# Narrower token rows, later weighting and later squares in a retention and HGRN2 step

## The chip, the cores and the metric

The kernel runs on one core of a Trainium2 chip. What counts is the device time of one execution in microseconds (us). Three executions of the kernel before took 1049.72, 1050.12 and 1050.17 us; their median, 1050.12 us, is the time that the change is measured against.

The engines are PE (TensorE, the matrix products; PEld is its loading of weights), DVE (VectorE), ACT (ScalarE), POOL (GpSimd) and SP (SyncE, which here only issues transfers). Each engine works through its own instructions in the order in which they stand, and an instruction that waits holds up all behind it on that engine. Transfers run on 16 DMA engines.

## The reference: what is computed

One mixer layer: normalise, project to eight groups of 512 columns, run two recurrences, weight their outputs, project back, and normalise once more with the final weights.

```python
h = rmsnorm(x, norm_g)
p = (h @ w_in).astype(jnp.float32)
rq, rk, rv, rg, hq, hf, hi, hgate = jnp.split(p, 8, axis=-1)
...
o_ret = head_rmsnorm(o_ret, ret_g) * jax.nn.silu(rg)
...
o_hg, s_hg_new = chunked_decay_recurrence(hq_act, kin, hi, logf, s_hg)
o_hg = head_rmsnorm(o_hg, hg_g) * jax.nn.silu(hgate)
o_cat = jnp.concatenate([o_ret, o_hg], axis=-1)
y = x + o_cat @ w_out
```

`head_rmsnorm` divides each head's output of 128 numbers by the root of its mean square. There are 2048 prompt tokens (width 1024, four heads of 128 for each recurrence) and eight further tokens that go through one decoding step. Every product of float32 matrices is made of three products of rounded halves: with x = xh + xl and w = wh + wl it is xh·wh + xl·wh + xh·wl.

## The kernel before, in words

**Stages.** Stage one (0 to 573 us) normalises the tokens and makes the value, query, key and gate projections and the retention. It goes over 24 blocks of 256 tokens (the eight blocks three times, once for each set of projections), and each block has seven products (`v_pair`, its matmuls in `three`, L352). Before the next block can be scaled, the squares of its tokens have to be summed: `stats_load` (L261) loads the 256 tokens in two halves j = 0 and 1, each as two tiles `xn` of 128x512; `stats_sum` (L267, ACT) squares and sums them; `stats_end` takes the root on POOL (L277, L111, L112); `spread_dg` (L288, DVE) puts the results on a diagonal `dg`, and PE spreads it with the matmul `prs` (L293). In the same stretch the gate weights are loaded (`wgr`, L519), combined on DVE (L505 to L508), stored (`ws1T`, L531) and multiplied with the decoding tokens (`pgd`, L592). The tiles of a pool are used in turn, so that a load into one waits for whatever last used it.

Stage two (573 to 851 us) makes the HGRN projections of the two halves of the tokens, four heads each (`seg_steps`, L996, into `pjfh` and `pjqh`), and runs the recurrence of each head one unit behind the projections. The tokens stand in four blocks of 512, split into `xh` and `xl` (`x_alloc`, `x_split`, L115 and L116), as tiles of 128 partitions x 8 rows of 528 elements, of which blocks 0, 2 and 3 fill 512 and block 1 fills 520 (512 and the eight decoding tokens). The recurrence works in levels (`plh`, L1208, L1253, L1258, and `pah`, L1226); between levels DVE multiplies `kh` and `qqh` (L1178, L1181) and copies a level's result into `Abh` (L1214). `tail_steps` then has, for the two groups of four chunks g = 0 and 1: `kt` (L1075, L1077), `uu` (matmul `puh`, L1083, state update L1091), `oo` (matmul `poh`, L1099 and L1101; squares of the outputs on ACT, L1105; the root on POOL, L111 and L112, into `orsh`; the weighting with root and gate on DVE, L1110, into `obh`) and `tr` (transpose `poth` on PE, L1117; `oth` on ACT, L1119; store to memory, L1120).

Stage three (851 to 1046 us) multiplies the outputs with `w_out`: four token blocks plainly (`py`, L1607) beside the last unit of the recurrence, and the rest with products of sums (`po`, L352). For that the weights are loaded (`wor`, L1476) and split into `woh` (ACT, L1481) and `wol` (DVE, L1482), and the outputs are loaded (`o_load`, L1492, tile `or`) and split into `oc_h` (ACT) and `oc_l` (DVE) by `o_split`. The values and gates of a unit come through four loads (`v`, L1023).

**What sets the order.** PE's order is written out. In stage one a table `after` says behind which of a block's seven products a step is issued. In stages two and three every step has a number between 0 and 1 within its unit, and `merge` puts the lists of steps (projections, levels, and `rest`) together by these numbers; in the last unit they are scaled to 0.57·at for the levels and 0.55 + 0.5·at for `rest`. The order on the other engines comes from a scheduler that may move an instruction ahead of others whose results it doesn't need. `behind(f)` ties what f issues: it is scheduled after the last instruction that DVE, ACT and SP had been given up to that point.

Of the kernel before, what the change touches and what calls it, by code (L numbers as in the profile page):

```python
# [11 lines left out]
F32R = mybir.dt.float32r  # L12
# [6 lines left out]
P = 128  # L19
D = 1024  # L20
KT = D // P
# [20 lines left out]
def step_kernel(ctx, tc, a, out):  # L42
# [67 lines left out]
    def rsqrt_mean(dst, src, n, eps):  # L110
        pool.tensor_scalar(dst, src, 1.0 / n, eps, op0=ALU.mult, op1=ALU.add)  # L111
        pool.tensor_tensor(dst, dst, mhalf[: dst.shape[0], : dst.shape[1]], op=ALU.pow)  # L112
# [11 lines left out]
    def behind(f):  # L124

        last = {}
        for i in reversed(nc.cur_bb.bb.instructions):
            if i.engine in (dve.engine, act.engine, sp.engine) and i.engine not in last:
                last[i.engine] = i
                if len(last) == 3:  # L130
                    break
        with ExitStack() as es:
            for i in last.values():
                es.enter_context(tc.issue_after(i))
            f()
# [40 lines left out]
    x_cur = {}  # L176
    x0p = []

    def x_alloc(blk):
        pl = x0p[0] if blk % 2 else xp  # L180
        x_cur[blk] = tuple(pl.tile([P, KT, 528], F32R, tag=f"x{t}{1 - blk % 2}", name=f"x{t}{blk}") for t in "hl")

    def x_load(blk, kp):
        r = rawp.tile([P, 2, 512], F32, tag="raw", name=f"xr{blk}{kp}")
# [72 lines left out]
    def stats_load(i, j):  # L257
        c = 2 * V_ORDER[i] + j
        st[i, j] = [vq.tile([P, GW], F32, tag="xn", name=f"xn{c}{h}", bufs=2) for h in range(2)]
        for h, r in enumerate(st[i, j]):  # L260
            sp.dma_start(r, a["x_prompt"][0, c * P : (c + 1) * P, h * GW : (h + 1) * GW])  # L261

    def stats_sum(i, j):
        if not j:
            st[i] = sm.tile([P, 4], F32, tag="ms", name=f"ms{V_ORDER[i]}")
        for h, r in enumerate(st[i, j]):
            act.activation(r, r, AF.Square, accum_out=st[i][:, 2 * h + j : 2 * h + j + 1])  # L267
# [618 lines left out]
    for i in range(2, n_tok):  # L886
        after = {n: [] for n in range(7)}
        m, j = i // N_V + 1, i % N_V
        if N_V <= i < 2 * N_V:
            after[3.5 if i > N_V + 1 else 4.5 if i > N_V else 5.5] = [q_flip]  # L890
        if N_V < i <= 2 * N_V:
            after.setdefault(2.5 if i < N_V + 3 else 1.5 if i < 2 * N_V else 2, []).append(q_flip)
        if i in (N_V, 2 * N_V):
            after[4 if i == N_V else 1] += [lambda m=i // N_V: wg_decode_turn(m)]
        if i == 2 * N_V:
            r_begin()
        if i >= 2 * N_V:
            for n, f in r_steps(i - 2 * N_V).items():
                after.setdefault(n, []).extend(f)
        if same(i + 1):  # L900
            for op in ("S1", "S2", "S3", "S4"):
                sop[i + 1, op] = sop[i, op]
        elif i + 1 < n_tok:
            if not spooled(i + 1):
                after[0] += [lambda i=i: spread_dg(i + 1)]
                after[1] += [lambda i=i: spread(i + 1)]
            tied = behind if i >= N_V - 1 else lambda f: f()
            late = 2 if same(i) else 0
            after[2 + late] += [
                lambda i=i, t=tied: t(lambda: tok_ops(i + 1)), lambda i=i, t=tied: t(lambda: s_split(i + 1, 0))  # L910
            ]
            after[4 + late // 2] += [lambda i=i, t=tied: t(lambda: s_split(i + 1, 1))]
        if i + 2 < n_tok and not same(i + 2):
            at = 5 if i % N_V > 2 else 2
            if same(i + 1):
                at = 6
            after[at] += [lambda i=i: tok_load(i + 2)]
        if i + 2 < N_V:
            after[1] += [lambda i=i: behind(lambda: stats_sum(i + 2, 0)), lambda i=i: stats_load(i + 2, 1)]
            after[4] += [lambda i=i: behind(lambda: stats_sum(i + 2, 1)), lambda i=i: stats_end(i + 2)]  # L920
            if i + 3 < N_V:
                after[5] += [lambda i=i: stats_load(i + 3, 0)]
        if N_V <= i + 1 < n_tok:
            after[4] += [lambda i=i: rot_load(i + 1)]
        if i == 2:
            after[0] += [decode_dg]
            after[2] += [decode_spread]
        if m < 3:
            if 2 <= j < 6:
                after[0] += [lambda m=m, k=j - 2: wg_load(m, k)]  # L930
                after[4] += [lambda m=m, k=j - 2: wg_decode(m, k), lambda m=m, k=j - 2: wg_spool(m, k)]
            if j == 7:
                after[0] += [lambda m=m: wg_decode_out(m)]
                for n, (_, op, _) in enumerate(CHAIN):
                    after[n] = [lambda m=m, op=op: wg_fetch(m, op)] + after[n]
        if i >= N_V - 1 and j in (7, 0) and i < n_tok - 1:
            for n, (_, op, _) in enumerate(CHAIN):
                if (n + SPLIT_AT) // 7 == (j + 1) % N_V:
                    after[3 if n == 6 else (n + SPLIT_AT) % 7] += [lambda op=op: behind(lambda: wg_split(op))]
        if i == 2 * N_V + 2:  # L940
            after[0] += [lambda: d_pad(0)]
        hd = i - 2 * N_V - 2
        if 0 <= hd < NH:
            after[3] += [lambda hd=hd: d_load(hd)]
            after[4] += [lambda hd=hd: behind(lambda: d_mul(hd, 0))]
            after[6] += [lambda hd=hd: behind(lambda: d_add(hd))]
        if 0 < hd <= NH:
            after[1] += [lambda hd=hd: d_mm(hd - 1)]
        if i == n_tok - 1:
            after[0] += [w_load]  # L950
            after[0] += [lambda: x_alloc(0), lambda: x_raw.update({(0, kp): x_load(0, kp) for kp in range(4)})]
            for kp, at in enumerate((1.5, 2.5, 3.5, 7)):
                if at > 6:
                    continue
                after.setdefault(at, [])
                after[at] += [lambda kp=kp: behind(lambda: x_split(0, kp, x_raw[0, kp]))]
            after[4] += [w_fetch]
        v_pair(i, after)
# [104 lines left out]
    def tail_steps(half, hd, acol, qcol, vcol, kT, decay, box, eps, gcol, name, ksb, ns):  # L1063
        ob = {}
# [28 lines left out]
        def oo(g):  # L1093
            st = st_tile()
            po = ps_o.tile([P, 4, P], F32, tag="o", name=f"po{name}{g}")
            for j in range(4):
                c = 4 * g + j
                src = box["old"] if c == 0 else st[:, (c - 1) % ns]
                pe.matmul(po[:, j], acol(c), vcol(c), start=True, stop=src is None)  # L1099
                if src is not None:  # L1100
                    pe.matmul(po[:, j], qcol(c), src, start=False, stop=True)  # L1101
            ms = sm.tile([P, 4], F32, tag="oms", name=f"oms{name}{g}")
            for j in range(4):
                jk = pools["tp"].tile([P, P], F32, tag="jk", name=f"jk{name}{g}{j}", bufs=1)
                act.activation(jk, po[:, j], AF.Square, accum_out=ms[:, j : j + 1])  # L1105
            rs = sm.tile([P, 4], F32, tag="ors", name=f"ors{name}{g}")
            rsqrt_mean(rs, ms, P, eps)
            ob[g] = pools["tp"].tile([P, 4, P], F32, tag="ob", name=f"ob{name}{g}", bufs=2)
            for j in range(4):
                dve.scalar_tensor_tensor(  # L1110
                    ob[g][:, j], po[:, j], rs[:, j : j + 1], gcol(4 * g + j), op0=ALU.mult, op1=ALU.mult
                )

        def tr(g):
            pt = ps_tr.tile([P, 4, P], F32, tag="tr", name=f"pot{name}{g}")
            for j in range(4):
                pe.transpose(pt[:, j], ob[g][:, j], ident)  # L1117
            ot = pools["tp"].tile([P, 512], F32, tag="ot", name=f"ot{name}{g}", bufs=2)
            act.activation(ot, pt.rearrange("p a b -> p (a b)"), AF.Copy, scale=ng[:, hd : hd + 1])  # L1119
            pool.dma_start(  # L1120
                o_dram[hd, :, half * HALF + g * 512 : half * HALF + (g + 1) * 512], ot
            )

        return dict(k0=lambda: kt(0), k1=lambda: kt(1), u0=lambda: uu(0), u1=lambda: uu(1),
                    o0=lambda: oo(0), o1=lambda: oo(1), t0=lambda: tr(0), t1=lambda: tr(1))

    def joined(*fs):
        def run():
# [12 lines left out]
    def hgrn_rec(half, h, u):  # L1141
        name = f"h{half}{h}"
# [135 lines left out]
        def last():  # L1278
            if half == 1:
# [3 lines left out]
                  (0.55, lambda: level(3, 0)), (0.68, lambda: level(3, 1)), (0.84, scores3),  # L1283
                  (0.95, t["k0"]), (0.98, t["k1"])]
        rest = [(0.02, begin), (0.13, t["u0"]), (0.28, t["u1"]), (0.43, t["o0"]), (0.47, t["o1"]),
                (0.6, t["t0"]), (0.73, t["t1"]), (0.73, last)]
        if half == 0:
            levels.insert(0, (0.0, lambda: collect(h, u)))
        return levels, rest
# [520 lines left out]
    for i in range(p0, n_pairs):  # L1810
        after = {}
# [98 lines left out]
```

## Time and profile before

| | us |
|---|---|
| median of three executions | 1050.12 (1049.72 to 1050.17) |
| the profiled execution | 1047.95 |
| its span, first to last instruction | 1046.2 |
| PE busy in the span | 1029.7 |
| DVE, ACT, POOL busy | 742.4, 552.6, 130.9 |
| DMA, mean over the span | 233 GB/s |
| granted TensorE clock | 0.999 |

The profiled execution lies 2.2 us below the median and 1.75 us above its own span. A row of a timeline gives the start and the length of an instruction, the engine, the line, the operation, the tiles out<-in, and in brackets how long the engine stood idle before it and what ended that. Neighbouring DVE and ACT instructions overlap by 0.07 to 0.1 us. In rows of waits, "1.5, 1, 1.5" is the total, the number of waits and the longest. "SPq" is SP's queue of transfers: start is when a transfer was issued, not when its data arrived.

### The profile page before, as it was taken

To read this page: it belongs to the slowest core of one execution; us is meant where nothing else is said; L and a number is where in the kernel's file an instruction comes from. 1 tells how busy PE (TensorE), PEld (TensorE's weight loads), DVE (VectorE), ACT (ScalarE), POOL (GpSimd) and SP (SyncE) were. 2 spreads that over 40 slices of the span, in tenths; PEclk is the share of its full clock that TensorE was granted. 3 is DMA by queue.
4 is the path that set the end of the run, shared out by engine and by line. 5 is a ranking of instruction groups with operands and counts; after the bars stand their busy time and mean duration, and the time that the engine had idled before them with its cause. 6 is when DMAs were issued, how large, how long until landed. Compare 5 with 4: busy or idle time off the path is not lost.

```text
span 1046.2 us, 21268 instructions
## 1 busy us (share of the span) xinstructions
PE 1029.7 (98%) x8231; PEld 851.1 (81%) x8231; DVE 742.4 (71%) x1372; ACT 552.6 (53%) x1208; POOL 130.9 (13%) x231
## 2 busy tenths in 40 slices
PE   9999999999999999999999999999999999999997
PEld 7777878887778888888888989897878877888775
DVE  6877567887655875666666776878767587578885
ACT  7954346644334865454555755575555474543241
POOL 0401001000000011111111100011022102311121
PEclk9999999999999999999999999999999999999999
DMA  8689989669876965767785785853876274475652
GB/s 296 210 315 353 312 321 338 244 233 319 274 252 195 328 232 173 195 217 232 217 266 159 260 304 181 271 190 123 269 244 223 67 232 135 155 290 201 232 174 101
DMA packets 145655, 244.08 MB, mean 233 GB/s; under 512 B 10801, under 2 KB 78657, under 8 KB 145425
## 3 DMA queue, kind: packets, MB, share of 16 engines
q1 hardware_dynamic: 137968, 217.68, 62.4%
q0 software_dynamic: 7440, 24.76, 6.2%
q8 instruction: 65, 1.06, 0.4%
q14 instruction: 38, 0.30, 0.1%
q10 hardware_dynamic: 144, 0.26, 0.1%
HBM read 160.22 MB, written 82.44 MB: 232 GB/s over the span
## 4 chain that ended last, share of the span: by engine, by line
PE 86%; DMA 4%; ACT 4%; DVE 4%; issue 1%; POOL 0%; SPq 0%; DVEq 0%; POOLq 0%; ACTq 0%
PE po L352 11%; PE pjfh L996 9%; PE pjqh L996 8%; PE py L1607 4%; PE plh L1208 2%; DMA xn<-in_x_prompt 1%; PE par L735 1%; PE puh L1083 1%; PE poh L1099 1%; PE pur L742 1%; PE por L748 1%; PE por L750 1%; PE poh L1101 1%; PE pv21a L352 1%; PE pv20a L352 1%
## 5 line engine op out<-in xcount | busy, mean ns | idle before, releaser
L1188 ACT ACTIVATE kepth<-kh 128x1024 f32<-128x1024 f32 x24 | 25.4, 1060 | 70.0 <-DVE kh L1178 70.0
L996 PE MATMUL pjfh<-xh,w_h 128*128 128x512 f32 (+2 forms) x160 | 60.2, 376 | 0.0
L996 PE MATMUL pjqh<-xh,w_h 128*128 128x512 f32 (+2 forms) x160 | 60.0, 375 | 0.0
L996 PE MATMUL pjqh<-xh,w_l 128*128 128x512 f32 (+2 forms) x160 | 55.9, 350 | 0.0
L996 PE MATMUL pjfh<-xl,w_h 128*128 128x512 f32 (+2 forms) x160 | 55.9, 349 | 0.0
L996 PE MATMUL pjfh<-xh,w_l 128*128 128x512 f32 (+2 forms) x160 | 55.9, 349 | 0.0
L996 PE MATMUL pjqh<-xl,w_h 128*128 128x512 f32 (+2 forms) x160 | 55.8, 349 | 0.0
L1178 DVE TENSOR_TENSOR kh<-kh,fph 128x512 f32<-128x512 f32 x48 | 33.3, 694 | 20.4 <-PE plh L1208 14.7
L116 DVE TENSOR_TENSOR ab_l<-xr,ab_h 128x512 fp32r<-128x512 f32 (+1 forms) x40 | 37.5, 953 | 9.5 <-ACT ab_h L115 9.5
L773 DVE SCALAR_TENSOR_TENSOR obr<-por,omr,rg 128x128 f32<-128x128 f32 x64 | 18.0, 344 | 31.5 <-POOL omr L765 26.8
L115 ACT ACTIVATE ab_h<-xr 128x512 fp32r<-128x512 f32 (+1 forms) x40 | 32.3, 838 | 15.0 <-DVE xr L306 15.0
L763 ACT ACTIVATE obr<-por 128x128 f32<-128x128 f32 x64 | 16.8, 277 | 42.9 <-PE por L750 39.4
L306 DVE SCALAR_TENSOR_TENSOR xr<-xr,g_in,rb 128x256 f32<-128x256 f32 x64 | 26.8, 477 | 15.9 <-DMA xr<-in_x_t 13.3
L1110 DVE SCALAR_TENSOR_TENSOR obh<-poh,orsh,v 128x128 f32<-128x128 f32 x64 | 18.0, 344 | 25.5 <-POOL orsh L112 25.4
L411 ACT ACTIVATE vo<-vo 128x512 f32<-128x512 f32 x32 | 20.1, 630 | 27.1 <-DVE vo L405 12.3
L996 PEld LDWEIGHTS pjqh<-xh,w_h 128*128 128x128 f32 x160 | 30.1, 188 | 5.0 <-issue 1.6
L996 PEld LDWEIGHTS pjfh<-xh,w_l 128*128 128x128 f32 x160 | 30.1, 188 | 4.2
L996 PEld LDWEIGHTS pjqh<-xh,w_l 128*128 128x128 f32 x160 | 30.1, 188 | 4.2
L996 PEld LDWEIGHTS pjfh<-xh,w_h 128*128 128x128 f32 x160 | 30.2, 189 | 3.8
L1181 DVE TENSOR_TENSOR qqh<-qqh,fph 128x512 f32<-128x512 f32 x48 | 32.7, 682 | 0.3 <-ACT kepth L1189 0.3
L996 PEld LDWEIGHTS pjfh<-xl,w_h 128*128 128x128 f32 x160 | 30.2, 189 | 2.7
L996 PEld LDWEIGHTS pjqh<-xl,w_h 128*128 128x128 f32 x160 | 30.2, 189 | 2.7
(1831 smaller groups left out, 3383.6 us busy)
## 6 DMA issues: line engine op xcount, KB each, us to landing
xr<-a_dram SPq DMA_DIRECT2D x24, 512.0 KB
S<-s_dram SPq DMA_DIRECT2D x24, 512.0 KB
xn<-in_x_prompt SPq DMA_DIRECT2D x32, 256.0 KB
xr<-in_x_t SPq DMA_DIRECT2D x16, 512.0 KB
a_dram<-xr SPq DMA_DIRECT2D x16, 512.0 KB
s_dram<-S SPq DMA_DIRECT2D x16, 512.0 KB
wgr<-in_w SPq DMA_DIRECT2D x16, 512.0 KB
xr<-a_dram SPq DMA_DIRECT2D x32, 256.0 KB
```

The lines of the kernel that those rows point to most:

```text
L115: act.activation(h, src, AF.Copy)
L116: dve.tensor_tensor(l, src, h.bitcast(F32), op=ALU.subtract)
L306: dve.scalar_tensor_tensor(r[:, k], r[:, k], g_in[:, kk : kk + 1], spread_to[i], op0=ALU.mult, op1=ALU.mult)
L352: pe.matmul(ps, xx, ww, start=(first and n == 0), stop=(last and n == 2), skip_group_check=more)
L411: act.activation(o, src, AF.Silu)
L773: dve.scalar_tensor_tensor(o[:, cc], po[:, h], ms[:, h : h + 1], rb_of[c, "g"][:, cc], op0=ALU.mult, op1=ALU.mult)
L996: pe.matmul(ps, ww[:, kk], x[:, k, b0 : b0 + n], start=(k == 0 and i == 0), stop=(k == KT - 1 and i == 2),)
L1178: dve.tensor_tensor(kv[:, :, 0, :], kv[:, :, 0, :], two[:, :, 1:2].to_broadcast([P, nb, b]), op=ALU.mult)
L1181: dve.tensor_tensor(qv[:, :, 1, :], qv[:, :, 1, :], two[:, :, 0:1].to_broadcast([P, nb, b]), op=ALU.mult)
L1188: act.activation(ss[:, 512:], k[:, :HALF], AF.Copy)
L1208: pe.matmul(dst[32 * i : 32 * i + 32, c], kk, qq, start=True, stop=True)
L1607: pe.matmul(ps, o[:, kk], w[:, k % 4, i * 512 : (i + 1) * 512], start=(k == 0 and n == 0), stop=(k == KT - 1 and n == 2),)
```

## The change

Three edits in one:

1. The tiles of the token blocks 0, 2 and 3 of stage two have rows of 512 elements in place of 528. Block 1 keeps 528.
2. In blocks 3, 4 and 5 of stage one, the squares of half 0 of the block after next, and behind them the load of half 1, are issued after the second following product (`after[2]`) in place of the first. Block 2 stays.
3. The weighting leaves `oo` and becomes a step of its own, `nn`, tied with `behind`. Its two groups stand at 0.53 and 0.59, where `oo` stood and stands at 0.43 and 0.47. The first transpose moves from 0.60 to 0.65.

```diff
-        x_cur[blk] = tuple(pl.tile([P, KT, 528], F32R, tag=f"x{t}{1 - blk % 2}", name=f"x{t}{blk}") for t in "hl")
+        x_cur[blk] = tuple(pl.tile([P, KT, 528 if blk == 1 else 512], F32R, tag=f"x{t}{1 - blk % 2}", name=f"x{t}{blk}") for t in "hl")
...
         if i + 2 < N_V:
-            after[1] += [lambda i=i: behind(lambda: stats_sum(i + 2, 0)), lambda i=i: stats_load(i + 2, 1)]
+            after[1 if i == 2 else 2] += [lambda i=i: behind(lambda: stats_sum(i + 2, 0)), lambda i=i: stats_load(i + 2, 1)]
             after[4] += [lambda i=i: behind(lambda: stats_sum(i + 2, 1)), lambda i=i: stats_end(i + 2)]
...
             rsqrt_mean(rs, ms, P, eps)
+            ob[g] = po, rs
+
+        def nn(g):
+            po, rs = ob[g]
             ob[g] = pools["tp"].tile([P, 4, P], F32, tag="ob", name=f"ob{name}{g}", bufs=2)
             for j in range(4):
                 dve.scalar_tensor_tensor(
...
-                    o0=lambda: oo(0), o1=lambda: oo(1), t0=lambda: tr(0), t1=lambda: tr(1))
+                    o0=lambda: oo(0), o1=lambda: oo(1), n0=lambda: behind(lambda: nn(0)), n1=lambda: behind(lambda: nn(1)), t0=lambda: tr(0), t1=lambda: tr(1))
...
-                (0.6, t["t0"]), (0.73, t["t1"]), (0.73, last)]
+                (0.53, t["n0"]), (0.59, t["n1"]), (0.65, t["t0"]), (0.73, t["t1"]), (0.73, last)]
```

Lines of the kernel after L1107 stand four further down in the changed kernel: the weighting is L1114, `poth` L1121, the copy into `Abh` L1218, `wol` L1486. Apart from `poth`, which moves back by six matmuls in seven of the eight units, PE's order stays.

Three places show how the other engines' orders move. First DVE in the fifth of the eight units (half 1, head 0), around the two weightings; `wot` are sums of output weights that are made on the side. Before:

```order
L1110 SCALAR_TENSOR_TENSOR obh_7620<-poh_7600,orsh_7617,v_7006 128x128 x4
L1311 TENSOR_TENSOR wot_7528<-wot_7527,wot_7526 128x512
L116 TENSOR_TENSOR xl_7368<-xr_7533,xh_7367 128x2x512
L1110 SCALAR_TENSOR_TENSOR obh_7655<-poh_7634,orsh_7652,v_7010 128x128 x4
L1313 TENSOR_TENSOR wot_7526<-wot_7526 128x512
L1053 TENSOR_TENSOR qqh_7503<-pjqh_0_7510,qsh_7661 128x512
L1214 COPY_PREDICATED Abh_7385<-lmask,plh_7673 128x16x8
L1055 TENSOR_TENSOR qqh_7503<-qqh_7503,fh_7501 128x512
```

After, on the same engine at the same place:

```order
L1315 TENSOR_TENSOR wot_7528<-wot_7527,wot_7526 128x512
L1053 TENSOR_TENSOR qqh_7503<-pjqh_0_7510,qsh_7651 128x512
L116 TENSOR_TENSOR xl_7368<-xr_7533,xh_7367 128x1024
L1317 TENSOR_TENSOR wot_7526<-wot_7526 128x512
L1055 TENSOR_TENSOR qqh_7503<-qqh_7503,fh_7501 128x512
L1319 TENSOR_TENSOR wot_7528<-wot_7527,wot_7526 128x512
L1114 SCALAR_TENSOR_TENSOR obh_7663<-poh_7600,orsh_7617,v_7006 128x128 x4
L1218 COPY_PREDICATED Abh_7385<-lmask,plh_7668 128x16x8
L1114 SCALAR_TENSOR_TENSOR obh_7708<-poh_7629,orsh_7647,v_7010 128x128 x4
```

Both weightings moved back, and the copy into `Abh` now stands between them and no longer behind both.

The second place is DVE at the end of stage two, where the second block of outputs (`or_9316`) is split. Before, the split stands in the middle of the last unit's levels:

```order
L116 TENSOR_TENSOR oc_l<-or_9180,oc_h 128x1024
L1482 TENSOR_TENSOR wol_9177<-wor_9166,woh_9176 128x1024
L1178 TENSOR_TENSOR kh_8516<-kh_8516,fph_8895 128x32x16
L1181 TENSOR_TENSOR qqh_8517<-qqh_8517,fph_8895 128x32x16
L1214 COPY_PREDICATED Abh_8920<-lmask,plh_9189 128x8x16
L116 TENSOR_TENSOR oc_l<-or_9316,oc_h 128x1024
L1178 TENSOR_TENSOR kh_8516<-kh_8516,fph_8895 128x16x32
```

After, DVE has it some twenty instructions later, behind the last projection:

```order
L1175 COPY dech_9416<-fph_9408 128x8
L1053 TENSOR_TENSOR qqh_9025<-pjqh_512_9320,qsh_9396 128x512
L1055 TENSOR_TENSOR qqh_9025<-qqh_9025,fh_9023 128x512
L116 TENSOR_TENSOR oc_l<-or_9316,oc_h 128x1024
L1486 TENSOR_TENSOR wol_9407<-wor_9318,woh_9406 128x1024
L1182 TENSOR_TENSOR kh_9024<-kh_9024,fh_9023 128x512
```

The split now comes directly before the subtraction `wol` of the fifth weight block, and on ACT its first half, `oc_h`, follows the activation `qsh` of that projection in the same way.

The third place is SP in block 3 of stage one, as a difference; `a_dram` and `s_dram` are stores of the scaled tokens and their sums, `v_dram` stores values:

```order
-L261 DMA xn_1009<-in_x_prompt 128x512
-L261 DMA xn_1010<-in_x_prompt 128x512
 L314 DMA a_dram_109<-xr_863 128x1024
 L314 DMA a_dram_109<-xr_864 128x1024
-L326 DMA s_dram_117<-S_4_1041 128x1024
-L326 DMA s_dram_117<-S_4_1042 128x1024
+L326 DMA s_dram_117<-S_4_1034 128x1024
+L326 DMA s_dram_117<-S_4_1035 128x1024
+L261 DMA xn_1049<-in_x_prompt 128x512
+L261 DMA xn_1050<-in_x_prompt 128x512
 L346 DMA v_dram_96<-vo_1080 128x512
```

The two loads of half 1 went from before four stores to behind them. Blocks 4 and 5 show the same.

## The prediction

> **What bounds the kernel now.** I read the page's shares first, then the chain, then PE's waits, and then the timelines around each wait.
>
> ```profile
> PE 1029.7 (98%) x8231; PEld 851.1 (81%) x8231; DVE 742.4 (71%) x1372; ACT 552.6 (53%) x1208; POOL 130.9 (13%) x231
> ...
> PE 86%; DMA 4%; ACT 4%; DVE 4%; issue 1%; POOL 0%; SPq 0%; DVEq 0%; POOLq 0%; ACTq 0%
> ```
>
> PE is busy for 1029.7 of 1046.2 us, and the change removes no matmul. So it can gain only where PE waits, or if the matmuls themselves get shorter. PE's waits that this change can touch:
>
> ```profile
> PE plh L1208 <- DVE Abh L1214: 1.5, 1, 1.5
> PE pah L1226 <- DVE qqh L1055: 1.3, 1, 1.3
> ...
> PE py L1607 <- DVE wol L1482: 1.0, 3, 0.4
> PE pgd L592 <- DMA wgr<-in_w: 0.8, 2, 0.6
> ...
> PE plh L1258 <- DVE qqh L1181: 0.4, 1, 0.4
> ```
>
> The view has 5.0 us in these five rows. That is the most that edits 2 and 3 together can win; what they can lose is not bounded this way.
>
> **Part 1, rows of 512.** No instruction is added or removed, and each step from one row to the next gets 64 bytes shorter. Two rows tell whether row length matters, each by the distance of starts:
>
> ```profile
> 837.68 0.39 PE L996 MATMUL pjfh<-xh,w_h 128*128 128x512 f32 x1
> ...
> 838.14 0.40 PE L996 MATMUL pjfh<-xh,w_l 128*128 128x512 f32 x1
> ```
> ```profile
> 852.68 0.40 PE L1607 MATMUL py<-wol,oc_h 128*128 128x512 f32 x1
> ...
> 854.30 0.39 PE L1607 MATMUL py<-woh,oc_l 128*128 128x512 f32 x1
> ```
> ```profile
> 949.68 0.39 PE L352 MATMUL po<-wol,op3S1h 128*128 128x512 f32 x1
> ...
> 951.49 0.39 PE L352 MATMUL po<-woh,op3S1h 128*128 128x512 f32 x1
> ```
>
> Reading from rows of 528, a 512-wide product takes (838.14 - 837.68)/2 = 0.230 us. `py`, which reads no such row, takes (854.30 - 852.68)/7 = 0.231, and `po` (951.49 - 949.68)/8 = 0.226. The slower pace thus also occurs without rows of 528, in a stretch that is likewise mixed with small matmuls. I take 0. The end of the range is a pace of `po` for all 512-wide products on those rows:
>
> ```profile
> L996 PE MATMUL pjfh<-xh,w_h x160: 276/392/500, 573.1 to 841.8; 128*128 128x512 f32 x96, 128*128 128x256 f32 x32, 128*128 128x264 f32 x32
> ...
> L116 DVE TENSOR_TENSOR xl<-xr,xh x16: 1212/1220/1226, 553.6 to 724.8; 128x1024 fp32r<-128x1024 f32 x16
> ...
> L116 DVE TENSOR_TENSOR oc_l<-or,oc_h x4: 1217/1221/1226, 840.7 to 887.4; 128x1024 fp32r<-128x1024 f32 x4
> ```
>
> There are six such groups, 6 x 96 = 576 products, x 0.004 to 0.005 us = up to 2.9 us. DVE's write into two pieces of 512 (`xl`) takes 1.220 us and into one piece of 1024 (`oc_l`) 1.221: nothing there. A loss has no row that speaks for it.
>
> **Part 2, squares a product later.** Two things follow in blocks 3 to 5. DVE reaches the sums of the gate weights sooner, and the second pair of token loads starts later.
>
> ```profile
> 122.41 0.68 DVE L507 TENSOR_TENSOR wgr<-wgr,wgr 128x512 f32<-128x512 f32 x1
> ```
> ```profile
> 124.52 5.08 DMA ws1T<-wgr
> 129.62 7.75 DMA wgr<-in_w
> ```
> ```profile
> 128.26 1.69 SPq L519 DMA_DIRECT2D wgr<-in_w  x2
> ```
>
> `ws1T` waits for L507, which ends at 123.09; its last store arrives at 129.60, and only then may the second load of `wgr` go out and keep PE waiting. With L506 and L507 each moved up past one split and the splits themselves earlier, L507 ends about 1.2 us sooner (one split of 1.22). The load can't use all of that: in SP's order it stands behind the first `wgr` load, issued at 128.26 and taking some 0.5. So it starts about 0.8 us sooner, and of the 0.8 us of waiting I credit 0.8 at most. Now the cost:
>
> ```profile
> 84.76 1.39 SPq L261 DMA_DIRECT2D xn<-in_x_prompt  x2
> ```
> ```profile
> 90.00 0.63 ACT L267 ACTIVATE xn<-xn 128x512 f32<-128x512 f32 x1 [0.37 <-DMA xn<-in_x_prompt]
> ```
> ```profile
> 98.26 0.45 POOL L277 TENSOR_TENSOR ms<-ms 128x2 f32<-128x2 f32 x1 [16.76 <-ACT xn L267]
> ...
> 99.40 0.69 POOL L112 TENSOR_TENSOR rs_all<-rs_all,mhalf 128x2 f32<-128x2 f32 x1
> ```
> ```profile
> 127.17 0.61 PE L293 MATMUL prs<-dg,ones 128*128 128x128 f32 x4
> ```
>
> A load of `xn` here took 90.00 - 84.76 = 5.2 us. In block 4 the second pair now goes out behind the `s_dram` stores, near 118.3, and arrives by about 123.0 to 123.5. Two squares take 1.2, POOL's three steps 99.40 + 0.69 - 98.26 = 1.8, two `dg` 0.5: done at 126.5 to 127.0, and `prs` needs it at 127.17. The spare time is 0.2 to 0.7 us here, a little more in block 3, less in block 5. I take 0.4 us lost in all three together and 0.8 gained: -0.4, with ends -0.8 and +0.4. The Trainium skill, "DMA: Bandwidth & Descriptors", section "Anatomy of one DMA — SWDGE (gpsimd) path", fits a transfer as 2.0 us and its bytes over 436 GB/s, which as an estimate makes 2.6 us for these 256 KB; by it the loss would be 0 and the sum 0.4 lower. The trace says 5.2 in this crowded stretch, and the page's fit is for one transfer from POOL's path.
>
> **Part 3, weighting.** In the unit of PE's longest wait:
>
> ```profile
> 720.09 0.68 DVE L1181 TENSOR_TENSOR qqh<-qqh,fph 128x512 f32<-128x512 f32 x1
> 723.20 1.13 DVE L1110 SCALAR_TENSOR_TENSOR obh<-poh,orsh,v 128x128 f32<-128x128 f32 x4 [2.43 <-POOL orsh L112]
> ...
> 729.21 0.28 DVE L1214 COPY_PREDICATED Abh<-lmask,plh 128x128 f32<-128x128 uint8 x1
> ```
> ```profile
> 721.65 1.07 ACT L115 ACTIVATE xh<-xr 128x1024 fp32r<-128x1024 f32 x1
> ```
> ```profile
> 722.14 1.03 POOL L112 TENSOR_TENSOR orsh<-orsh,mhalf 128x4 f32<-128x4 f32 x1
> ...
> 725.06 1.87 POOL L112 TENSOR_TENSOR orsh<-orsh,mhalf 128x4 f32<-128x4 f32 x1
> ```
> ```profile
> 729.54 0.74 PE L1208 MATMUL plh<-qqh,kh 128*32 128x16 f32 x64 [1.50 <-DVE Abh L1214]
> ```
>
> DVE stands idle behind `obh` for 2.43 us, and both weightings come ahead of `Abh`, for which PE waits from 728.04 on. After: DVE fills that time with `wot` and `qqh`, can start `xl` when `xh` is done at 722.72, ends it at 723.94, has three operations of 0.68 behind it (725.98), one weighting (1.13: 727.1) and `Abh` (727.4). That is 0.6 us before 728.04: the wait goes, -1.5. The second weighting and what is behind it on DVE then run in time that PE doesn't watch; `poth` needs the first at 727.4 or later. Ends: -1.5 and 0.
>
> At the end of stage two the split `oc_l` of the second output block, and ahead of it `oc_h` on ACT, move from a place with slack into the stretch where DVE has no gap:
>
> ```profile
> 844.36 1.22 DVE L116 TENSOR_TENSOR oc_l<-or,oc_h 128x1024 fp32r<-128x1024 f32 x1
> ...
> 856.46 1.22 DVE L1482 TENSOR_TENSOR wol<-wor,woh 128x1024 fp32r<-128x1024 f32 x1
> ```
> ```profile
> 854.49 0.60 ACT L1052 ACTIVATE qsh<-pjqh 128x512 f32<-128x512 f32 x1
> ```
> ```profile
> 852.22 0.38 SPq L1492 DMA_DIRECT2D or<-o_dram  x1
> ```
> ```profile
> 896.36 1.05 PE L1083 MATMUL puh<-v,ksh 128*128 128x128 f32 x8
> ```
>
> DVE's run around the `wol` of 856.46 and behind it, for which `py` waits three times, gets 1.14 us longer (1.22 less the overlap). It starts some 0.4 us sooner, because ACT is rid of `oc_h` (1.06 us) ahead of `qsh`, though part of that goes to waiting for the later weightings. The 0.4 us wait for `qqh` (L1181) goes as well, but lies ahead of the same run and is no gain of its own. Net +0.7; ends +0.1 (ACT keeps all of it) and +1.1. The same move delays transfers: `or` for the third block now waits for `oc_l` and goes out near 857.3 in place of 852.22, and SP has the four value loads of the last unit behind it. PE first needs those at 896.36, so 39 us cover it: 0.
>
> In the last unit two more operations stand ahead of the second weighting:
>
> ```profile
> 914.70 1.12 DVE L1110 SCALAR_TENSOR_TENSOR obh<-poh,orsh,v 128x128 f32<-128x128 f32 x4 [1.18 <-POOL orsh L112]
> ```
> ```profile
> 915.89 0.60 PE L1117 MATMUL poth<-ident,obh 128*128 128x128 f32 x4
> ```
>
> They fit into the 1.18 us of idle time almost, but POOL's root then runs beside a busy DVE, which by 725.06 against 722.14 costs up to 0.8. There is no slack before `poth`: +0.3, ends 0 and 0.9. In the other six units I find `Abh`, `obh` and `poth` no later than PE asks for them.
>
> **Sum:** 0 - 0.4 - 1.5 + 0.7 + 0.3 = -0.9 us. The profiled execution, 1047.95, would become 1047.05; it lies 2.2 below the median, so against 1050.12 I get 1049.2. The ends without part 1 are -2.2 and +0.9, thus 1047.9 to 1051.0.
>
> **Rivals.**
>
> *Late squares (slower).* If the moved `xn` loads take longer than about 5.5 us, `prs` waits in three blocks, and squares that stand on ACT ahead of the evictions of the next product hold these up too. Half-megabyte loads of the same stretch took 7.75 us; with that, 3 x (7.75 - 5.5) = 6.8, and halfway there 3.4 in place of -0.4: sum +2.9, 1053.0. For it: the queue is shared with stores that now go first. Against: the loads are half as large.
>
> *POOL slowed (no change).* If POOL's roots take over 3 us longer while DVE works without pause, `obh` and `Abh` come as late as before; the 1.5 stays and the sum is +0.6, 1050.7. For it: 1.87 against 1.03. Against: two such delays make under 2 us. The Trainium skill, "SBUF — State Buffer", says that a DVE instruction with two SBUF inputs contends with a GpSimd instruction that reads SBUF and that one blocks the other fully; the rows agree in sign, with 0.84 us more.
>
> *Rows count (faster).* -2.9 on top: -3.8, 1046.3. For it: 0.230 against 0.226. Against: `py` at 0.231.
>
> **Chances.** Forecast 0.44, late squares 0.22, POOL 0.16, rows 0.18. 0.2% of the median, 2.1 us, is about what a measurement tells from no change; faster means under 1048.0. Rows give 0.18 of it and the low end of the forecast 0.12: 0.30. Slower is late squares: 0.22. The same: 0.48. The forecast's own range is 1047.9 to 1051.0; to leave out no more than 2 in 10 the range goes to the rivals' middles, 1046.3 to 1053.0.
>
> **What would show it.** Right: no wait of PE for `Abh` in the fifth unit, a wait for `wgr` under 0.3 us, `wol` waits of PE that end later by less than 1.1 us, L996 still at 0.230. Wrong: waits for `prs` or for ACT's evictions near 106, 127 and 148 us; waits of `poth` for `obh`; or the 1.5 us coming back at the next level. The weakest step is the landing of `xn`, which a trace of another order can't show.

## The result, and the profile after

| | before | after |
|---|---|---|
| median of the runs on the same chip, us | 1050.12 (1049.28 to 1052.62, 7 runs) | 1046.84 (1045.61 to 1048.71, 7 runs) |
| ratio, 95% interval | 1 | 0.9973 (0.9964 to 0.9983) |
| the profiled execution, us | 1047.95 | 1047.01 |
| its span, us | 1046.2 | 1045.2 |

By the ratio the changed kernel is faster by 0.27%, 2.8 us (1.8 to 3.8). The forecast was 1049.2, no change. The two profiled executions differ by only 0.94 us. That pair hides part of the gain, and the first thing to learn from this case is why.

PE's waits in the profile after (total in us, number of waits, longest):

```profile
PE pv2b L352 <- DVE ab_l L116: 1.6, 1, 1.6
PE py L1611 <- DVE wol L1486: 1.5, 3, 0.8
PE pah L1230 <- DVE qqh L1055: 1.4, 1, 1.4
...
PE pv L352 <- ACT wv_h L115: 1.0, 1, 1.0
...
PE pv8a L352 <- ACT u L392: 0.5, 1, 0.5
PE pgd L592 <- DMA wgr<-in_w: 0.5, 1, 0.5
PE py L1611 <- ACT woh L1485: 0.3, 1, 0.3
```

The wait of `plh` for `Abh` (1.5 before) and that for `qqh` in front of the last level (0.4 before) are gone. The waits of `py` for `wol` grew from 1.0 to 1.5, and one for `woh` of 0.3 is new. At the top stands a wait near 60 us that the change can't reach, since up to there the instruction streams are identical: `pv2b` for `ab_l`. Before, it was

```profile
PE pv2b L352 <- DVE ab_l L116: 0.7, 1, 0.7
```

To separate such accidents from the change, I took the start of the same PE instruction in two profiles, counted from the first of each, and followed how the difference to the profile before moves from place to place. In us, negative is earlier:

| stretch of the span before, us | after | a second profile after | what lies there |
|---|---|---|---|
| 0 to 118 | +0.67 | -0.53 | `pv`, `pv2b`, `pv3a`; block 3 of edit 2, without a wait |
| 118 to 145 | -0.39 | -1.02 | `wgr`, edit 2 |
| 145 to 575 | +0.64 | +1.67 | other waits of stage one |
| 575 to 722 | -0.36 | -0.36 | projections on rows of 512 |
| 722 to 735 | -1.64 | -1.65 | fifth unit, `Abh` |
| 735 to 843 | -0.45 | -0.44 | projections on rows of 512 |
| 843 to 851 | -0.56 | -0.57 | last level, `qqh` |
| 851 to 867 | +1.13 | +1.13 | `pah`, `wol` |
| 867 to 1035 | +0.02 | +0.02 | stage three |

From 575 us on the two profiles of the changed kernel agree within 0.02 us at each place, and sum up to -1.86 and -1.87. Up to 575 us they don't agree: PE's waits of stage one, some of them for transfers (`wgr`), differ from execution to execution (`pv2b` 1.6 and 0.7 us in these two), and a stretch by a microsecond and more. So stages two and three can be read from single profiles to some hundredths, stage one cannot.

**Edit 3, fifth unit.** DVE, then PE, in timelines of the profile after:

```profile
723.83 1.22 DVE L116 TENSOR_TENSOR xl<-xr,xh 128x1024 fp32r<-128x1024 f32 x1
...
726.77 1.12 DVE L1114 SCALAR_TENSOR_TENSOR obh<-poh,orsh,v 128x128 f32<-128x128 f32 x4
727.81 0.28 DVE L1218 COPY_PREDICATED Abh<-lmask,plh 128x128 f32<-128x128 uint8 x1
728.01 1.11 DVE L1114 SCALAR_TENSOR_TENSOR obh<-poh,orsh,v 128x128 f32<-128x128 f32 x4
```
```profile
727.96 0.60 PE L1121 MATMUL poth<-ident,obh 128*128 128x128 f32 x4
728.49 0.74 PE L1212 MATMUL plh<-qqh,kh 128*32 128x16 f32 x64
```

`Abh` ends at 728.09, between the two weightings, and `plh` starts at 728.49 with no wait in brackets. `poth` needs the first weighting, done at 727.89, and starts at 727.96 without a wait either.

**Edit 3, end of stage two.** DVE and SP:

```profile
853.04 0.69 DVE L1053 TENSOR_TENSOR qqh<-pjqh,qsh 128x512 f32<-128x512 f32 x1 [1.55 <-ACT qsh L1052]
853.77 0.69 DVE L1055 TENSOR_TENSOR qqh<-qqh,fh 128x512 f32<-128x512 f32 x1
854.38 1.22 DVE L116 TENSOR_TENSOR oc_l<-or,oc_h 128x1024 fp32r<-128x1024 f32 x1
855.52 1.22 DVE L1486 TENSOR_TENSOR wol<-wor,woh 128x1024 fp32r<-128x1024 f32 x1
```
```profile
855.63 0.38 SPq L1496 DMA_DIRECT2D or<-o_dram  x1
```

The split `oc_l` stands where the order showed it, ahead of `wol`, and the next load of `or` goes out at 855.63 in place of 852.22. No PE wait for the last unit's values follows.

**Edit 2, block 4 of stage one.** SP, ACT, DVE and PE:

```profile
119.06 2.13 SPq L261 DMA_DIRECT2D xn<-in_x_prompt  x2
```
```profile
124.10 0.63 ACT L267 ACTIVATE xn<-xn 128x512 f32<-128x512 f32 x1 [0.91 <-DMA xn<-in_x_prompt]
```
```profile
122.12 0.68 DVE L507 TENSOR_TENSOR wgr<-wgr,wgr 128x512 f32<-128x512 f32 x1
```
```profile
126.81 0.48 DVE L288 TENSOR_SCALAR dg<-ident,rs_all 128x128 f32<-128x128 f32 x2 [2.80 <-POOL rs_all L112]
```
```profile
127.84 0.61 PE L293 MATMUL prs<-dg,ones 128*128 128x128 f32 x4
```

The moved pair of loads goes out at 119.06 and ACT has it at 124.10: 5.04 us, nearly what was taken from the trace before. `dg` ends at 127.29, 0.55 us before `prs` starts; in blocks 3 and 5 it ends 1.6 and 1.1 us before. PE doesn't wait for `prs` in any profile of this study.

**Edit 1, and the end of the last unit.** The group of `pjfh`, and the last weighting with its transpose:

```profile
L996 PE MATMUL pjfh<-xh,w_h x160: 277/389/504, 574.0 to 840.2; 128*128 128x512 f32 x96, 128*128 128x256 f32 x32, 128*128 128x264 f32 x32
```
```profile
913.54 1.13 DVE L1114 SCALAR_TENSOR_TENSOR obh<-poh,orsh,v 128x128 f32<-128x128 f32 x4
```
```profile
914.95 0.60 PE L1121 MATMUL poth<-ident,obh 128*128 128x128 f32 x4
```

This group mixes three widths; its median is 389 ns, and was 392. For the 576 products of 512 columns of all six groups alone, the traces give a median of 393 ns, and 395 before; from one start to the next it is 231, and was 233. The weighting ends at 914.67, 0.28 us before `poth`.

### The profile page after: what moved, and what is told of

Read it like the earlier page. It is cut to its first block, busy times and chain, and to the rows that moved or that the text cites. A ratio compares the mean times of both kernels' runs of the same rounds, so it can differ in the third digit from the quotient of the medians.

```text
span 1045.2 us, 21267 instructions
## 1 busy us (share of the span) xinstructions
PE 1028.8 (98%) x8231; PEld 851.2 (81%) x8231; DVE 743.6 (71%) x1372; ACT 553.3 (53%) x1208; POOL 129.8 (12%) x231
## 4 chain that ended last, share of the span: by engine, by line
PE 79%; DMA 3%; ACT 2%; DVE 2%; issue 1%; SPq 1%; POOL 0%; DVEq 0%; POOLq 0%; ACTq 0%
PE po L352 11%; PE pjfh L996 8%; PE pjqh L996 8%; PE py L1611 4%; PE plh L1212 2%; PE puh L1083 1%; DMA T3l<-ws1T 1%; PE poh L1099 1%; PE pur L742 1%; PE par L735 1%; PE por L748 1%; PE por L750 1%; PE poh L1101 1%; PE pv21a L352 1%; PE pv20a L352 1%
## 5 line engine op out<-in xcount | busy, mean ns | idle before, releaser
L1114 DVE SCALAR_TENSOR_TENSOR obh<-poh,orsh,v 128x128 f32<-128x128 f32 x64 | 18.0, 343 | 14.2 <-POOL orsh L112 14.2
```

## The experiments

All ratios are against runs of the kernel before on the same chip. "Shift" is the movement of PE's starts against the profile before, read as in the table above.

### One edit at a time

Each is the kernel before with one of the three edits of the diff above and nothing else: the rows of 512, then the later squares, then the weighting.

> Only edit 1, the rows of 512. Theory of the prediction: no effect, 1050.1 within 0.3 us, the step of a 512-wide L996 product stays as before. Rival, that rows count: the profile of the changed kernel shows PE gaining steadily, 0.8 us in all between 573 and 850 us, and a median step of 231 in place of 233 ns; then this kernel alone gains 0.8 us, 1049.3, and its L996 step is 231 ns.

> Only edit 2, the later squares. Theory: the second wait of PE for the gate weights near 137 us (0.6 us) shrinks and nothing else in stage one depends on it: 0.4 us faster, 1049.7, PE's waits near 59, 79 and 193 us are chance and differ from run to run. Rival, that the new wait near 193 us in the profile of the changed kernel (1.0 us with its surroundings) comes from this edit: 0.6 us slower, 1050.7.

> Only edit 3, the later weighting. Theory: the wait for Abh in the fifth unit goes (-1.6 us), the one for qqh near 847 goes (-0.5), and the split of the second output block, moved into DVE's run at 856 us, costs 1.1: together -1.0, 1049.1. Rival, that the weighting carries the whole measured gain: -2.8, 1047.3.

| | time, us | ratio | shift 118 to 145 | 575 to 722 | 722 to 735 | 735 to 843 | 843 to 851 | 851 to 867 |
|---|---|---|---|---|---|---|---|---|
| rows_only | 1047.32 | 0.9994 (0.9985 to 1.0004) | +0.26 | -0.40 | -0.01 | -0.39 | -0.03 | +0.08 |
| squares_only | 1047.68 | 0.9990 (0.9982 to 0.9999) | -0.62 | 0.02 | 0.03 | 0.01 | 0.01 | 0.02 |
| weight_only | 1048.25 | 0.9994 (0.9982 to 1.0006) | -0.10 | -0.04 | -1.58 | 0.01 | -0.47 | +1.05 |

Of the three intervals only that of the squares leaves out 1, and by little. But the shifts take the change apart, each from a single profile. The rows act only in the two stretches of projections, and on nothing else: -0.8 us. The weighting wins 1.58 and 0.47 and loses 1.05: -1.0. The squares move nothing behind 575 us. The wait near 193 us that the rival of squares_only names (`pv8a`) is 0.2 us in that profile. It also stands, with 0.55 us, in the profile of no_squares below, so it isn't bound to edit 2. In the group of `pjfh` with rows_only:

```profile
L996 PE MATMUL pjfh<-xh,w_h x160: 277/389/499, 573.1 to 841.0; 128*128 128x512 f32 x96, 128*128 128x256 f32 x32, 128*128 128x264 f32 x32
```

### Is it the length of the row?

The kernel before, with the rows of blocks 0, 2 and 3 at 520:

```diff
-        x_cur[blk] = tuple(pl.tile([P, KT, 528], ...
+        x_cur[blk] = tuple(pl.tile([P, KT, 528 if blk == 1 else 520], ...
```

> Kernel before with rows of 520 elements for the token blocks 0, 2 and 3. Theory A, that a row's start counts (2080 bytes is no multiple of 512): median step of the 512-wide L996 products 233 ns as with 528. Theory B, that the length counts: 232 ns, halfway to 231 at 512. PE's waits stay as before.

```profile
L996 PE MATMUL pjfh<-xh,w_h x160: 276/394/502, 572.7 to 841.5; 128*128 128x512 f32 x96, 128*128 128x256 f32 x32, 128*128 128x264 f32 x32
```

One execution took 1047.75 us. The shifts are +0.14 and 0.00 in the two stretches of projections, and the products of 512 columns alone have a median of 395 ns and 233 from start to start, as with 528: 520 is as slow. (The 394 of this group, which mixes widths, is no sign of more; the other five have 391 to 392.) Each product reads 512 columns in all three kernels, so a shorter step from row to row does nothing by itself; that the row starts are multiples of 2048 bytes, and not of 2080 or 2112, is what the fast one has. Whether another multiple would do, and whether it is the start or something else about the place of the tile, wasn't tried.

### What the tie is worth

The changed kernel with the weightings at their new places, but not tied:

```diff
-  n0=lambda: behind(lambda: nn(0)), n1=lambda: behind(lambda: nn(1)),
+  n0=lambda: nn(0), n1=lambda: nn(1),
```

> The changed kernel with the weighting late but not tied. In its order half of the first weighting stands ahead of the side work again, and Abh still stands ahead of the second weighting. Theory, that Abh's place ahead of the second weighting is what counts: most of the 1.6 us stays won, and PE waits at most 0.6 us for Abh. Rival, that the tie is what counts, since DVE idles for orsh again: the wait is back at over 1 us.

One execution took 1047.34 us. The shift from 722 to 735 is -1.38 in place of -1.64, and the other places behind 575 us lie within 0.16 of the changed kernel. The later place carries most of the gain, and the tie adds 0.26 us of it there. Over all places behind 575 us this one profile wins 1.3 us, against the 1.9 with the tie.

### Undoing the loss at the end of stage two

The changed kernel, with load and split of the second output block given numbers in the last unit instead of standing at the end:

```diff
-  (7.48, lambda: o_split(0)), (7.8, lambda: o_load(1)),
+  (7.48, lambda: o_split(0)), (7.5, lambda: o_load(1)), (7.62, lambda: o_split(1)),
...
-    o_split(1)
     wo1[0]()
```

> The changed kernel with the split of the second output block (oc_h on ACT, oc_l on DVE) issued earlier, at 7.62 of the side list, so that it runs near 845 us again. Theory: the three waits of PE for wol shrink from 2.7 us of stall back to 1.6, and the kernel is 1.1 us faster than the changed one: 1045.7. Rival, that the weight splits bound this stretch whatever stands there: no change, 1046.8.

1046.78 us, ratio 0.9978 (0.9967 to 0.9989). PE's waits:

```profile
PE pah L1230 <- DVE qqh L1055: 2.3, 1, 2.3
...
PE py L1611 <- DVE wol L1486: 1.0, 3, 0.4
```

The waits for `wol` went back to 1.0, as wanted, and the wait for `pah` grew from 1.4 to 2.3. The shift from 851 to 867 is +0.92, against +1.13: a gain of 0.2 where 1.1 was expected. `oc_h` now lengthened ACT's run in front of `qsh`, from which `qqh` and with it `pah` come. So the split was to go into gaps of ACT and DVE, ACT's half tied ahead of `oth` near 836 and DVE's half near 845:

```diff
+                if name == "h11" and g == 0:
+                    es.enter_context(tc.issue_after(oc1_at[0]))
                 act.activation(ot, pt.rearrange("p a b -> p (a b)"), ...
...
-  (7.48, lambda: o_split(0)), (7.8, lambda: o_load(1)),
+  (7.47, lambda: o_load(1)), (7.48, lambda: o_split(0)),
+  (7.53, lambda: (oc1.extend(o_halves(1)), oc1[0]())), (7.65, lambda: oc1[1]()),
```

> The changed kernel with the split of the second output block early, but its ACT half (oc_h) tied into ACT's idle time of 2.9 us ahead of oth near 836 us, and its DVE half near 845 us. Theory after the run with the early split: ACT's unbroken run up to qsh and DVE's run behind it are both bounds of this stretch, and the block must leave both. Then PE's wait for qqh stays at 1.3 to 1.4 us in place of 2.3, the waits for wol stay at 1.0, and the stretch is 0.9 to 1.1 us shorter than in the changed kernel. Rival, that DVE's run alone is the bound: no better than the early split, 0.2 us.

1046.68 us, ratio 0.9978 (0.9967 to 0.9989): no gain over the changed kernel. The wait for `pah`, forecast at 1.3 to 1.4, is 2.1. In timelines of ACT, DVE and PE:

```profile
839.75 1.06 ACT L1511 ACTIVATE oc_h<-or 128x1024 fp32r<-128x1024 f32 x1 [5.06 <-PE pjfh L996]
...
849.71 1.68 ACT L1280 ACTIVATE Ah<-Abh 32x256 f32<-32x256 f32 x4
851.42 1.08 ACT L1079 ACTIVATE ksh<-pkh 128x512 f32<-128x512 f32 x2
852.39 0.60 ACT L1052 ACTIVATE qsh<-pjqh 128x512 f32<-128x512 f32 x1
```
```profile
853.02 0.69 DVE L1053 TENSOR_TENSOR qqh<-pjqh,qsh 128x512 f32<-128x512 f32 x1 [0.80 <-ACT qsh L1052]
```
```profile
854.50 0.65 PE L1238 MATMUL pah<-qqh,kh 128*32 128x64 f32 x32 [2.10 <-DVE qqh L1055]
```

In the changed kernel the same three stand at

```profile
849.73 1.69 ACT L1272 ACTIVATE Ah<-Abh 32x256 f32<-32x256 f32 x4
851.44 1.09 ACT L1077 ACTIVATE ksh<-pkh 128x512 f32<-128x512 f32 x2
852.41 0.60 ACT L1052 ACTIVATE qsh<-pjqh 128x512 f32<-128x512 f32 x1
```

The starts are equal within 0.02 us, but not for one reason. Near 843 us PE is 1.17 us further ahead in the profile of split_idle than in that of the changed kernel, all of it from stage one. Counted from PE, `qsh` thus comes 1.15 us later, about the length of `oc_h`. The split did not get into the gap: ACT stood idle in front of `oc_h` for 5.06 us, until PE released it with a product of `pjfh`. By the kernel, `oc_h` takes its tile from a pool of three (`wh`) that also holds the weights of these products. From there to `qsh` ACT has no pause, so that `oc_h` and what stands behind it lengthen the run after all, while DVE waits 0.8 us for `qsh`. So it is ACT's run that sets `pah`. What a split in a true gap would give isn't shown.

### Do the parts add up?

The changed kernel once more, on the chip of rows520, untied and split_idle.

> The changed kernel as it is, on the chip of the run beside it, for comparison: faster than before by the sum of the three parts as the traces show them, 0.5 (squares) + 0.8 (rows) + 1.0 (weighting) = 2.3 us, ratio 0.9978. If the three parts worked on one another, the ratio lies outside 0.9968 to 0.9988.

1046.23 us, ratio 0.9974 (0.9962 to 0.9985), the same as the first result. The three ratios of one edit each multiply to 0.9978, with an uncertainty of 0.0017 (their intervals added in squares). So the parts add up as far as the times can tell, and no effect of one on another shows. Its shifts are the second column of the first table.

### ACT's run: what goes behind `qsh`

Four of the copies ahead of `qsh` write the diagonal blocks of `Ah`, which PE reads only at 869.83 (`poh`, in the profile after). They were moved behind the first weight part of stage three, in the changed kernel, in split_idle, and in the kernel before:

```diff
+            def diag():
                 for i in range(4):
                     pp = slice(32 * i, 32 * i + 32)
                     act.activation(A[pp, :, pp], box["Ab"][pp], AF.Copy)
+
+            if name == "h12":
+                diag_late.append(diag)
+            else:
+                diag()
...
+        (0.025, lambda: behind(diag_late[0])),
         (0.03, wo1[1][2]), (0.07, wo1[1][3]),
```

> The changed kernel with one more edit: the four diagonal copies into Ah (L1272, 1.7 us on ACT) of the seventh unit are issued behind the first weight part of stage three, in place of ahead of ksh and qsh. Theory: the wait of PE for pah near 853 is set by ACT's run without a gap from 842.8 up to qsh, not by DVE, and what ACT does there for later use can go behind qsh. Then qsh starts at 850.4 or earlier in place of 852.4, DVE ends qqh (L1055) near 852.7 in place of 854.4, PE's wait for pah of 1.4 us falls to 0.1 or less, and DVE's run behind it (oc_l, wol) starts as much earlier, so that nothing is given back: 1.4 to 1.6 us less than the changed kernel, a ratio to the kernel before of 0.996 (0.995 to 0.997). Rival: DVE's run is the bound all the same and PE waits as much more for wol: pah gone, but the three waits for wol 2.5 to 3 us in place of 1.5, and the ratio stays at 0.9974.

> The split put into idle time (split_idle) with the four copies into Ah behind qsh as well. Theory (ACT's run sets qsh): qsh near 850.8, then DVE's products fph up to 852.2 are the later bound, qqh ends near 853.5, the wait for pah falls from 2.1 to 1.0-1.1 us; ratio about 0.9967. Rival (DVE's run is the bound): the wait for pah stays near 2 or the waits for wol grow by the same, ratio 0.9978 as before.

> The kernel before with only the four copies into Ah behind qsh. Theory: ACT's run bounds qsh in the kernel before too (854.5), so the wait for pah of 1.3 us falls to 0.2 or less; DVE starts L1053 near 854.0 in place of 855.1, and the waits for wol shorten rather than grow: 1.2 us from 848 to 870. Rival: no shift, or given back at wol.

| | time, us | ratio | shift 843 to 851 | 851 to 867 | 867 to 1035 |
|---|---|---|---|---|---|
| ah_late | 1043.77 | 0.9954 (0.9941 to 0.9967) | -0.54 | -0.94 | +0.41 |
| ah_late_idle | 1045.13 | 0.9965 (0.9952 to 0.9978) | -0.14 | -0.63 | +0.03 |
| before_ah_late | 1046.33, one execution | | 0.00 | -1.56 | +0.02 |

ACT, then DVE, with ah_late:

```profile
848.63 0.58 ACT L1054 ACTIVATE qsh<-pjqh 128x512 f32<-128x512 f32 x1
...
850.06 1.06 ACT L115 ACTIVATE oc_h<-or 128x1024 fp32r<-128x1024 f32 x1
...
851.96 1.67 ACT L1276 ACTIVATE Ah<-Abh 32x256 f32<-32x256 f32 x4
```
```profile
849.25 0.69 DVE L1055 TENSOR_TENSOR qqh<-pjqh,qsh 128x512 f32<-128x512 f32 x1
...
849.99 0.69 DVE L1057 TENSOR_TENSOR qqh<-qqh,fh 128x512 f32<-128x512 f32 x1
...
851.15 1.22 DVE L116 TENSOR_TENSOR oc_l<-or,oc_h 128x1024 fp32r<-128x1024 f32 x1
...
852.37 1.22 DVE L1495 TENSOR_TENSOR wol<-wor,woh 128x1024 fp32r<-128x1024 f32 x1
```

This execution was 1.1 us ahead of the profile after at 851 us anyway, from stage one. `qsh` starts 3.8 us sooner, 2.7 more than that, because the scheduler then also put it ahead of `ksh`. `qqh` is done at 850.68 in place of 854.46, and the wait for `pah` is no longer in the list of waits. The `wol` of 855.52 now starts at 852.37, so the waits behind don't grow:

```profile
PE py L1620 <- DVE wol L1495: 1.5, 3, 0.8
```

The stretch from 851 to 867 got 2.07 us shorter than in the changed kernel (1.13 + 0.94), a little more than the 1.4 to 1.6 expected; 0.4 are given back behind 867. This kernel is faster than both: 0.46% below the kernel before (0.33 to 0.59%), 4.8 us by the ratio. Against the changed kernel on its own chip (0.9974) the ratio is lower by 0.0020, with an uncertainty of 0.0017. In the kernel before the same edit gives 1.56 us, where 1.2 was expected: the wait for `pah` is gone, and those for `wol` stay at 1.0 and don't shrink as expected. In split_idle it gives 1.4 over the whole stretch behind 575 us, and a wait for `pah` of 0.3 stays, where 1.0 to 1.1 was expected:

```profile
PE pah L1240 <- DVE qqh L1057: 0.3, 1, 0.3
```

### What edit 2 is worth

The changed kernel with the squares back at `after[1]`:

```diff
-            after[1 if i == 2 else 2] += [...
+            after[1] += [...
```

> The changed kernel with the squares of blocks 3 to 5 back where they stood (edits 1 and 3 alone). By PE's starts in stages two and three these two edits give 1.85 us, so a ratio of 0.9982 if edit 2 is worth about a microsecond, as its own times said (0.9990, interval 0.9982 to 0.9999). Rival: what edit 2 wins near 136 us is lost again at waits between 190 and 450 us, as the single profiles suggest, so that it is worth nothing: then 0.9974 as with all three, or under. In the profile: waits for wgr near 136 us of 0.6 to 1.0 us in all, as before.

1046.08 us, ratio 0.9969 (0.9956 to 0.9981). That is no slower than with all three edits (0.9973, 0.9974), so the rival has the better number. At the place itself the edit does what it says; in the profile of no_squares the wait stands as in the profile before:

```profile
PE pgd L592 <- DMA wgr<-in_w: 0.8, 2, 0.6
```

The eight profiles with edit 2 show shifts of -0.39 to -1.02 from 118 to 145 us, on average -0.8; the five without it -0.10 to +0.26, on average +0.1. From 145 to 575 us, where nothing was edited, the first group loses 0.6 to 3.0 us, and the second 0.1 to 0.3 in four cases and 1.7 in the fifth, no_squares. Thus the loss there isn't bound to edit 2, but the gain may not last either. From the start to 575 us together, the eight profiles are 0.2 us later on average than the profile before and the five 0.1 us later, within a spread of -0.6 to +1.8: no gain of edit 2 shows there. Part of it may turn up as a later wait for the same tile. In four of the eight, and in none of the five, PE waits 0.2 to 1.5 us for `wgr` near 260 us, as in after_again, where it doesn't wait near 137:

```profile
259.74 0.62 PE L592 MATMUL pgd<-wgr,pk 128*8 128x256 f32 x8 [0.56 <-DMA wgr<-in_w]
```

That the one wait leads to the other wasn't tested. By its own times edit 2 is worth -1.0 us (0.1 to 1.9 of gain); by the difference to no_squares +0.5, uncertain by 1.6 (the intervals of both added in squares). Its worth in the whole stays open.

## Why the prediction was right or wrong

The range, 1046.3 to 1053.0, held the time, the point was 2.4 us too high, and "faster by over 0.2%" had 0.30 against 0.48 for no change. That the profiled execution came out at 1047.01, where 1047.05 was forecast, is luck: it lost more in stage one, up to 118 us and behind 145, than its pair before.

**Part 1, rows: wrong.** The step "I take 0" failed. It measured -0.8, inside its end of -2.9. The comparison of 0.230 us for the old rows with 0.231 for `py` set two steps against seven and looked for a difference of 1.4 ns (0.8 us over 576 products), which starts rounded to 10 ns can't show over two steps; and `py` has other neighbours. The rival *Rows count* had the sign, with 2.9 for 0.8: its end took the pace of `po` for that of the products on short rows. Over all pairs of neighbouring products of 512 columns, `po` has a median of 227 ns from start to start, and the products on short rows 231. The trace before held more than the two rows: over all such pairs, the median was 233 for the old rows and 230.5 for `py`. What part of that the rows make up it couldn't say, but it was no ground for taking 0.

**Part 2, squares: the mechanism was right, its size is open.** `xn` took 5.04 us where 5.2 was taken, so that `prs` has 0.55 us to spare, within the 0.2 to 0.7 of the sum. No 0.4 us were lost there, and *Late squares* didn't come. L507 ends at 122.80 in place of 123.09; since PE is 0.67 us later at this place in the profile after, that is 1.0 us sooner, and 1.2 was forecast. A wait for `wgr` of 0.5 stays there, above the 0.3 named as right. At the place PE won 0.4 to 1.0, against 0.4 forecast. What the whole run gets of it isn't settled.

The Trainium skill, "DMA: Bandwidth & Descriptors", section "Anatomy of one DMA — SWDGE (gpsimd) path", gave 2.6 us as an estimate for one such load. The trace doesn't agree: the 5.04 us here, from issue to use, are again about twice that. How much of it comes from the other traffic and how much from the path (SP's queue in place of POOL's), no run here shows.

**Part 3, weighting: right but for the last unit.** The wait for `Abh`: -1.5 forecast, -1.64. At the end of stage two: +0.7 forecast, and -0.56 + 1.13 = +0.57 measured, with the 0.4 us wait for `qqh` gone ahead of the loss, as the text had it. The working held as well: counted from PE's starts at 843 us, `qsh` came 0.55 us sooner (854.49 and 852.41, of which 1.53 lie ahead of 843), where 0.4 was taken, and DVE's run behind it got longer by the split. What the sum didn't see is that ACT's run in front of `qsh` sets the wait for `pah`, while DVE's sets the waits for `wol`; the runs with the split elsewhere and with the copies behind `qsh` show it. The last unit: +0.3 forecast, 0.0 measured, since `obh` ends 0.28 us ahead of `poth`; the step that failed is the slower root on POOL. It took 1.01 us beside a DVE without pause, as it had taken beside an idle one, and the two operations that moved ahead of the weighting fit into DVE's idle time, so that `obh` starts 0.04 us after the root:

```profile
912.49 1.01 POOL L112 TENSOR_TENSOR orsh<-orsh,mhalf 128x4 f32<-128x4 f32 x1
```

**POOL slowed** didn't come: in the fifth unit the second root took 1.33 us, not more than the 1.87 of before, beside a DVE without pause.

```profile
725.18 1.33 POOL L112 TENSOR_TENSOR orsh<-orsh,mhalf 128x4 f32<-128x4 f32 x1
```

The Trainium skill, "SBUF — State Buffer", section "Who interferes with whom", has a DVE instruction with two SBUF inputs and a GpSimd instruction that reads SBUF contend. The 1.33 us against the first root's 1.03 agree in sign, the last unit's 1.01 doesn't. The delay of 0.3 us didn't reach PE.

**The sum.** In PE's starts -0.8 (rows) and -1.0 (weighting) are sure, and -0.4 to -1.0 at the place of edit 2 came in every profile that has it. That makes -2.2 to -2.8, or -2.3 to -2.9 with the -1.86 of both together, against the measured -2.8 (-3.8 to -1.8), if the last part lasts. Without any gain of edit 2 the -1.86 still lies within that interval, at its near end. The forecast of -0.9 was short by the rows (0.8), the last unit (0.3), 0.3 in the weighting's other two terms, and by whatever edit 2 gives beyond 0.4. One end was added up wrongly: the upper one, +0.9, keeps the -1.5 of `Abh`, for which the text gives 0 as an end; with that it is +2.4, or 1052.5, still inside the range.

## What to carry to other kernels

A cost that is multiplied by hundreds of instructions can't be set to zero from a handful of rows: 1.4 ns on 576 products is 0.8 us, and needs the median of the whole group or an experiment. Where an engine without a gap feeds the waiting one, work that goes in front of that wait only moves it; look instead for what on that engine is needed late, and put it behind (1.69 us of copies, read 18 us later, were worth 1.4 to 1.8 us of PE's starts here in three kernels, more than all of edit 3). An absolute time in two profiles compares nothing until the shift ahead of it is taken off. Where waits change from execution to execution, compare profiles place by place, and trust only the places that repeat.

## What the runs showed of the hardware that had not been expected

- Products of 512 columns read from rows that start every 2048 bytes took a median of 393 ns in the records and 231 from start to start, from rows every 2080 or every 2112 bytes 395 and 233. By PE's starts the first is worth 0.8 us in 576 products, and the second nothing.
- In two profiles of one kernel, PE's starts in stages two and three agreed within 0.02 us at each of six places, while stage one differed by 1.2 us up to 118 us and by 1.0 in the other direction behind 145, with identical instructions.
- The same POOL operation (`orsh`, 128x4) took 1.01 us in the last unit, beside an idle DVE (before) and beside a DVE without pause (after), and 1.87 and 1.33 us in the fifth unit.
